# A hybrid decoder layer: low parts of weights kept in DRAM, more raw tiles at the turn into down, and tiles of its own for a layer norm

## The chip, the cores and the metric

The kernel runs on one core of a Trainium2 chip (trn2). The metric is the device time of one execution in microseconds (us); the time before is the median of three executions. A TensorE matmul (PE) multiplies a 128 x 128 stationary piece of a weight by a moving tile of 128 x 512; VectorE is called DVE, ScalarE ACT, GpSimd POOL and SyncE SP. SP issues most transfers, POOL the others, each from a queue that it takes in order.

## What is computed

One layer over 2048 positions of width 1024, all in float32. A conditioning vector gives shifts, scales and gates. The mixer has two branches, a state-space scan and a gated convolution with a layer norm behind it, both fed by one input projection and joined by one output projection; a dense squared-ReLU network follows.

```python
h = rmsnorm(x, norm_mix_w) * (1 + sc_mix) + sh_mix
z, xbc, dt_raw, glu_a, glu_b = split(h @ w_in)
y = gated_rmsnorm(ssd(silu(dwconv4(xbc)), dt_raw), z)
u = dwconv31(glu_a * sigmoid(glu_b))
u = silu(layernorm(u, cf_ln_w, cf_ln_b))
x = x + g_mix * (concat([y, u]) @ w_out)
h = rmsnorm(x, norm_mlp_w) * (1 + sc_mlp) + sh_mlp
x = x + g_mlp * (square(relu(h @ w_mlp1)) @ w_mlp2)
out = rmsnorm(x, norm_final_w)
```

## The kernel before

**Products in two parts.** Every float32 matrix is split into a high and a low part that TensorE takes at its fast rate: ACT copies the raw tile into a rounded tile (hi), and DVE subtracts that from the raw tile (lo). A product is three matmuls, hi x hi, hi x lo and lo x hi, added in PSUM. `split_w` does this for a weight block: it loads 128 x 1024 values (512 KB) by SP into one of three raw tiles (wr0, wr1, wr2, in turn), has ACT write hi into one of two tiles wh (L296) and DVE write lo into one of two tiles wl (L297). The raw tile is free when DVE has done L297, a wh and a wl tile when TensorE has finished the block that used them.

**Stages.** The 2048 positions are two halves of 1024, each of two quarters of 512 (Q).
- Mixer, half 0 (to 550 us) and half 1 (to 1000 us): 36 blocks of w_in, 48 matmuls each, are multiplied with both quarters of the half (L306 to L308), the scan and the convolution run beside that. `conv_cf` filters the gated values (31 taps, DVE) and stores v to v_d in DRAM.
- Output projection (`mix`, `mix_q`), a quarter at a time: 16 blocks of w_out with 24 matmuls each (L854 to L856), the results gated and added to x. The first two quarters run from 1009 to 1190 us, the last two from 1868 to 2047 us.
- `up` of half 0 (1191 to 1500 us), `down_` of half 0 (1502 to 1867 us), quarters three and four, `up` of half 1 (2047 to 2366 us), `down7` of half 1 (2366 to 2690 us).

So every block of w_in is split twice, and every block of w_out four times.

**The layer norm of the convolution** is a generator, `ln_cf`, that other stages advance by `ln_step`. For each of four pieces of 256 positions it loads v by POOL into two tiles cu, sums them on DVE (L410 to L413), sums over the partitions on PE (L416), subtracts the mean, squares, takes the root, scales, applies ACT's silu and stores the result from the cu tiles to m_d (L435). The sums stand in tiles ca. The convolution's filter uses cu and ca as well. For half 0 `mix` takes a step per block; for half 1 `down_` does, in its last k-block, a step per m.

**up** makes seven-product combinations of 2 x 2 weight blocks (`w1_prep`): of raw tiles x and y it forms the sums s and u in tp0 and tp1 (L985 to L987), and splits the combinations (L885 is ACT's copy, L886 DVE's subtraction, L1003 to L1005 the product's matmuls). When L987 has read y, the next y is loaded into the same tile. In half 1 `keep_ops` also forms sums of the results in tiles tt and stores seven operands per unit to op_d in DRAM, by POOL.

**down7** reads those operands again (`op_raw`, two loads per operand, in the three raw tiles) and takes weight combinations of w2 from `w2_prep`, whose first sum also stands in a tile tt. Its first operands are fetched by the generator `ahead`, advanced by `up` in its last units. The eight accumulators are loaded from x2_d with each pair of product groups.

**Who sets the order.** The statements are written in this order, with generators advanced at the places named; each engine's instructions are then placed by a scheduler, so a small move in the source can move an instruction several places on its engine. `urgent` raises the priority of a split.

## Time and profile before

| what | value |
|---|---|
| median of three executions | 2706.15 us (2704.84 to 2707.09) |
| profiled execution, its own time | 2701.98 us |
| its span | 2699.8 us |
| mean granted clock of TensorE | 0.992 |
| TensorE busy | 2634.3 us, 98% |
| VectorE busy | 2181.0 us, 81% |
| ScalarE busy | 1400.4 us, 52% |
| GpSimd busy | 300.2 us, 11% |
| read from DRAM, written | 304.65 MB, 100.93 MB |

The profile is that of one execution. Its time is 4.17 us below the median. Busy time is the time in which an engine worked on an instruction; a group of instructions is named by the line of the kernel, the engine, the operation and the tiles (out<-in). A wait is put down to the instruction or transfer that came last. The granted clock is a share of full speed: 1.00 is 2.4 GHz and 0.50 is 1.2 GHz. "DMA to landing" is the time from the issue of a transfer to its last byte.

### The profile page before, as it was taken

To read this page: it belongs to the slowest core of one execution; us is meant where nothing else is said; L and a number is where in the kernel's file an instruction comes from. 1 tells how busy PE (TensorE), PEld (TensorE's weight loads), DVE (VectorE), ACT (ScalarE), POOL (GpSimd) and SP (SyncE) were. 2 spreads that over 40 slices of the span, in tenths; PEclk is the share of its full clock that TensorE was granted. 3 is DMA by queue.
4 is the path that set the end of the run, shared out by engine and by line. 5 is a ranking of instruction groups with operands and counts; after the bars stand their busy time and mean duration, and the time that the engine had idled before them with its cause. 6 is when DMAs were issued, how large, how long until landed. Compare 5 with 4: busy or idle time off the path is not lost. (4 is left out here: it accounts for less than half of the span.)

```text
span 2699.8 us, 34186 instructions
## 1 busy us (share of the span) xinstructions
PE 2634.3 (98%) x12460; PEld 2149.7 (80%) x12460; DVE 2181.0 (81%) x3368; ACT 1400.4 (52%) x2169; POOL 300.2 (11%) x469
## 2 busy tenths in 40 slices
PE   7999999999999999999999999999999999999997
PEld 4778888788788778888888888878888778778886
DVE  7889999998996668999999874466547776588886
ACT  5757546676754755546566312354336445554452
POOL 1320120030021000011011000000001222100000
PEclk9999999999999999999999999999999999999998
DMA  7463233232322356545434733355735554564541
GB/s 288 140 214 109 79 102 110 86 111 79 118 86 78 123 177 231 164 161 188 148 137 141 242 111 100 109 195 181 244 122 188 204 197 148 197 212 146 167 148 63
DMA packets 130921, 407.82 MB, mean 151 GB/s; under 512 B 15937, under 2 KB 24769, under 8 KB 130753
## 3 DMA queue, kind: packets, MB, share of 16 engines
q1 hardware_dynamic: 97728, 294.07, 32.7%
q0 software_dynamic: 33024, 111.57, 11.6%
q8 instruction: 98, 1.61, 0.2%
q14 instruction: 71, 0.57, 0.1%
HBM read 304.65 MB, written 100.93 MB: 150 GB/s over the span
## 5 line engine op out<-in xcount | busy, mean ns | idle before, releaser
L306 PE MATMUL mm<-big,wh 128*128 128x512 f32 x1024 | 411.3, 402 | 2.4 <-DVE tp L716 1.8
L308 PE MATMUL mm<-big,wl 128*128 128x512 f32 x1024 | 403.9, 394 | 0.0
L307 PE MATMUL mm<-big,wh 128*128 128x512 f32 x1024 | 400.3, 391 | 0.0
L296 ACT ACTIVATE wh<-wr 128x1024 fp32r<-128x1024 f32 x167 | 176.1, 1055 | 314.5 <-PE mm L855 114.0
L297 DVE TENSOR_TENSOR wl<-wr,wh 128x1024 fp32r<-128x1024 f32 x167 | 203.6, 1220 | 70.1 <-ACT wh L296 59.2
L306 PEld LDWEIGHTS mm<-big,wh 128*128 128x128 f32 x1024 | 192.3, 188 | 51.9 <-issue 9.2
L308 PEld LDWEIGHTS mm<-big,wl 128*128 128x128 f32 x1024 | 192.3, 188 | 43.6 <-issue 3.2
L307 PEld LDWEIGHTS mm<-big,wh 128*128 128x128 f32 x1024 | 192.4, 188 | 42.9 <-issue 4.7
L1003 PE MATMUL mm<-big,wh 128*128 128x512 f32 x536 | 212.3, 396 | 9.1 <-ACT wh L885 3.7
L1004 PE MATMUL mm<-big,wh 128*128 128x512 f32 x536 | 210.7, 393 | 0.0
L1005 PE MATMUL mm<-big,wl 128*128 128x512 f32 x532 | 207.2, 389 | 1.2 <-DVE wl L886 1.2
L856 PE MATMUL mm<-big,wl 128*128 128x512 f32 x512 | 200.1, 391 | 1.4 <-DVE wl L297 1.4
L854 PE MATMUL mm<-big,wh 128*128 128x512 f32 x512 | 200.0, 391 | 0.4 <-ACT wh L296 0.4
L855 PE MATMUL mm<-big,wh 128*128 128x512 f32 x512 | 199.3, 389 | 0.0
L1349 PE MATMUL mm<-big,wh 128*128 128x512 f32 x496 | 194.9, 393 | 0.0
L1351 PE MATMUL mm<-big,wl 128*128 128x512 f32 x496 | 194.0, 391 | 0.3 <-DVE wl L297 0.3
L1350 PE MATMUL mm<-big,wh 128*128 128x512 f32 x496 | 194.1, 391 | 0.0
L387 DVE SCALAR_TENSOR_TENSOR ca<-cu,const,ca 128x512 f32<-128x512 f32 x240 | 178.6, 744 | 1.5 <-ACT ca L381 1.2
L390 DVE SCALAR_TENSOR_TENSOR ca<-ca,const,ca 128x512 f32<-128x512 f32 x240 | 178.3, 743 | 0.0
L1005 PE MATMUL mm<-big,wh 128*128 128x512 f32 x440 | 173.3, 394 | 0.0
L1003 PE MATMUL mm<-big,wl 128*128 128x512 f32 x436 | 170.3, 391 | 1.5 <-ACT cc L1113 1.2
L389 DVE SCALAR_TENSOR_TENSOR ca<-cu,const,ca 128x513 f32<-128x513 f32 x224 | 167.2, 746 | 3.7 <-ACT ca L383 3.7
(346 smaller groups left out, 5919.4 us busy)
## 6 DMA issues: line engine op xcount, KB each, us to landing
wr<-in_w_dram SPq DMA_DIRECT2D x120, 512.0 KB, 3.5
wr<-in_w_in_dram SPq DMA_DIRECT2D x72, 512.0 KB, 3.4
wr<-in_w_out_dram SPq DMA_DIRECT2D x64, 512.0 KB, 4.1
wr<-op_d SPq DMA_DIRECT2D x56, 512.0 KB, 4.6
ca<-in_w_ada_dram POOLq DMA_DIRECT2D x64, 256.0 KB, 3.5
tp<-ac_d SPq DMA_DIRECT2D x32, 512.0 KB, 4.3
wr<-m_d SPq DMA_DIRECT2D x32, 512.0 KB, 4.2
op_d<-tt POOLq DMA_DIRECT2D x64, 256.0 KB, 2.6
```

What stands on the lines that cost most here:

```text
L297: V.tensor_tensor(lo, raw, f(hi), SUB)
L306: T.matmul(ps, lhsT=hi[:, c], rhs=a[:, 0, :], start=(k == 0), stop=False)
L307: T.matmul(ps, lhsT=hi[:, c], rhs=a[:, 1, :], start=False, stop=False)
L308: T.matmul(ps, lhsT=lo[:, c], rhs=a[:, 0, :], start=False, stop=(k == KT - 1))
L854: T.matmul(ps, lhsT=hi[:, c], rhs=a[:, 0, :], start=(pos + k == 0), stop=False)
L855: T.matmul(ps, lhsT=hi[:, c], rhs=a[:, 1, :], start=False, stop=False)
L856: T.matmul(ps, lhsT=lo[:, c], rhs=a[:, 0, :], start=False, stop=(pos == 1 and k == KT - 1))
L1003: T.matmul(ps, lhsT=hi[:, k], rhs=xs[kp][:, 0, :], start=new and kp == 0, stop=False, skip_group_check=True)
L1004: T.matmul(ps, lhsT=hi[:, k], rhs=xs[kp][:, 1, :], start=False, stop=False, skip_group_check=True)
L1005: T.matmul(ps, lhsT=lo[:, k], rhs=xs[kp][:, 0, :], start=False, stop=kp == KP - 1, skip_group_check=True)
L1349: T.matmul(ps, lhsT=whl[0][:, c], rhs=hi, start=(k == 0), stop=False)
L1350: T.matmul(ps, lhsT=whl[0][:, c], rhs=lo, start=False, stop=False)
```

## The change

Three things are changed, and one goes with them.

1. `split_w` gets a key. At the first use of each of 52 blocks (36 of w_in, 16 of w_out) DVE makes lo as before, and POOL stores it to DRAM (lo_d). At the 84 later uses SP loads lo from there into the wl tile, in place of DVE's subtraction. The raw tile is then free when ACT has written hi.
2. The layer norm gets two tiles lv for v and two tiles la for its sums, in place of cu and ca. For half 1 its steps in `down_` come only at odd m, eight fewer, and the rest are taken by `mix` of half 1, a step per block.
3. In `w1_prep` of half 1 the sums of every second unit stand in cu0 and cu1 instead of tp0 and tp1.
4. At the turn into `down7` the raw operands have five tiles (wr0 to wr2, or0 and or1), the first operand is asked for before the first weights, and `ahead` splits three of them and asks for a fourth; the accumulators are loaded one or two at a time in another order; the first sum of `w2_prep` stands in a tile ca instead of tt.

The changed line numbers are about 15 higher: L1001 to L1003 are L985 to L987 of before, L902 is L886, L1119 and L1131 are L1103 and L1115 (DVE's part of a result of up), L989 is L974 (raw loads), L296 the raw load of `split_w`, L301 the load of lo, and L1259 the accumulator load.

Six more calls change from `split_w(w_in[b])` to `split_in(b)` (L514, L570, L581, L651, L806, L816); the rest, cut to its core:

```diff
-    def split_w(src, dst=None):
+    lo_d = {}
+    def split_w(src, dst=None, key=None):
         raw = t_wr()
...
             A.activation(hi, raw, AF.Copy)
+            if key in lo_d:
+                nc.sync.dma_start(f(lo), lo_d[key])
+                return hi, lo
             V.tensor_tensor(lo, raw, f(hi), SUB)
+        if key:
+            lo_d[key] = t_dr([P, D], f"lo_d{len(lo_d)}")
+            nc.gpsimd.dma_start(lo_d[key], f(lo))
         return hi, lo
+    def split_in(b, dst=None):
+        return split_w(w_in[b], dst, ("in", b))
...
         for j in range(2):
-            v = t_cu([P, 4, W])
+            v = t_turn("lv", 2, [P, D]).rearrange("p (a b) -> p a b", a=4)
             nc.gpsimd.dma_start(v, v_d[q // 2][:, 4 * j : 4 * j + 4, (q % 2) * 2 + i].rearrange("p k two n -> p k (two n)"))
...
             yield
-        sa = t_ca().rearrange("p (j w) -> p j w", w=W)
+        sa = t_turn("la", 2, [P, Q]).rearrange("p (j w) -> p j w", w=W)
         V.tensor_tensor(sa, vs[0][:, 0:2, :], vs[0][:, 2:4, :], ADD)
...
             V.tensor_tensor(vs[j], vs[j], mu[:, None, :].to_broadcast([P, 4, W]), SUB)
-        sq = t_ca().rearrange("p (j w) -> p j w", w=W)
+        sq = t_turn("la", 2, [P, Q]).rearrange("p (j w) -> p j w", w=W)
         for j in range(4):
...
         n = 0
-        ws = [w_out[m, pos if q % 2 else 1 - pos] for mg in (0, 4) for pos in range(2) for m in range(mg, mg + 4)]
+        ws = [(m, pos if q % 2 else 1 - pos) for mg in (0, 4) for pos in range(2) for m in range(mg, mg + 4)]
+        def weights(n):
+            return split_w(w_out[ws[n]], key=ws[n])
         if whl is None:
-            whl = split_w(ws[0])
+            whl = weights(0)
         for mg in (0, 4):
...
                     if n < 16:
-                        whl = split_w(ws[n])
+                        whl = weights(n)
                     side(n - 1)
...
             tick()
-            if half == 0:
-                ln_step(0)
+            ln_step(half)
             if n in (6, 7, 8, 9, 12, 13, 14, 15):
...
-    def w1_prep(sums0):
+    def w1_prep(half):
+        sums0 = plan[half][7]
         x, y = r2(t_raw(w1[0], "wr0")), r2(t_raw(w1[1], "wr1"))
...
                 if n == 2:
-                    s, u = (r2(t_at(t)) for t in (("tp0", "tp1") if mp else sums0))
+                    s, u = (r2(t_at(t)) for t in (sums0 if mp == 0 else ("cu0", "cu1") if half and mp % 2 else ("tp0", "tp1")))
                     V.tensor_tensor(s, y[:, 0:1, :].to_broadcast([P, 2, Q]), x, SUB)
...
         early(half, hx, second)
-        prep = w1_prep(plan[half][7])
+        prep = w1_prep(half)
         ws = [next(prep), next(prep)]
...
+        rot = [0]
         def op_raw(kb, n):
-            return [t_raw(op_d[kb][n][:, h * D : (h + 1) * D]) for h in range(2)]
+            rot[0] += 2
+            return [t_raw(op_d[kb][n][:, h * D : (h + 1) * D], ("wr0", "wr1", "wr2", "or0", "or1")[(rot[0] + h) % 5]) for h in range(2)]
...
+        def acc_load(m):
+            acc[m] = t_at(("tp7", "tp5", "tp4", "tp6", "cu0", "cu1", "state", "ac")[m])
+            nc.sync.dma_start(acc[m], x2_d[1][m])
         def ahead():
+            raws = {0: op_raw(0, 0)}
+            next(prep)
+            yield
+            raws[1] = op_raw(0, 1)
+            yield
+            op_split(0, raws[0])
+            acc_load(0)
+            acc_load(2)
+            yield
+            raws[2] = op_raw(0, 2)
             ws.extend((next(prep), next(prep)))
             yield
-            raws = op_raw(0, 0)
-            yield
-            op_split(0, raws)
+            op_split(1, raws[1])
             ws.append(next(prep))
-            raws = op_raw(0, 1)
-            yield
-            op_split(1, raws)
-            raws = op_raw(0, 2)
+            yield
+            raws[3] = op_raw(0, 3)
+            op_split(2, raws[2])
             ws.append(next(prep))
-            yield
-            op_split(2, raws)
-            raws = op_raw(0, 3)
-            yield
-            op_split(3, raws)
-            yield
+            ready.update(raws)
+            yield
+        ready = {}
...
                     for n in range(7):
-                        if kb == 0 and g == 0 and 4 <= n:
-                            op_split(n, op_raw(0, n))
+                        if kb == 0 and g == 0 and 3 <= n:
+                            op_split(n, ready[n])
+                        if kb == 0 and g == 0 and 2 <= n < 6:
+                            ready[n + 1] = ready.get(n + 1) or op_raw(0, n + 1)
+                        if kb == 0 and g == 0 and n == 0:
+                            acc_load(1)
+                            acc_load(3)
+                        if kb == 0 and g == 0 and 2 <= n < 6:
+                            acc_load(n + 2)
                         if g == 1:
...
                             mp = 2 * g + l
-                            if kb == 0 and n == 0:
-                                for m in (2 * mp, 2 * mp + 1):
-                                    acc[m] = t_at(f"tp{4 + m}" if m < 4 else ("cu0", "cu1", "state", "ac")[m - 4])
-                                    nc.sync.dma_start(acc[m], x2_d[1][m])
                             if n == 0:
...
                     src[l].update(a21=y[:, 0, :], a12=y[:, 1, :])
+                if kb == 0 and g == 0:
+                    yield
                 for n in range(7):
...
                         if n == 2:
-                            s["s1"] = t_turn("tt", 4, [P, Q])
+                            s["s1"] = t_ca()
                             V.tensor_tensor(s["s1"], s["a21"], s["a22"], SUB)
...
                     tick()
-                    if half == 0:
+                    if half == 0 and m % 2:
                         ln_step(1)
-                    if half == 0 and m % 2:
                         nxt += mix_prep(2, len(nxt), plan[1][0])
```

**SP in the third quarter of the output projection.** Before, SP's queue holds the raw loads alone (L293), each waiting for DVE, which has read the raw tile:

```order
L293 DMA wr1_2273_15389<-in_w_out_dram 128x1024 [waits DMAHW7_49,DVE_49]
L293 DMA wr2_2261_15312<-in_w_out_dram 128x1024 [waits DMAHW5_49,DVE_49]
L293 DMA wr2_2277_15434<-in_w_out_dram 128x1024 [waits DMAHW1_49,DMAHW0_49,DVE_49]
L293 DMA wr0_2281_15476<-in_w_out_dram 128x1024 [waits DMAHW4_49,DVE_49]
L293 DMA wr1_2285_15518<-in_w_out_dram 128x1024 [waits DMAHW7_49,DMAHW3_49,DVE_49]
```

Now a load of lo (L301) stands beside each raw load (L296); it waits for TensorE, the raw load for ScalarE:

```order
L296 DMA wr2_2256_15388<-in_w_out_dram 128x1024 [waits DMAHW1_49,DMAHW6_49,DVE_49,Activation_49]
L301 DMA wl1_2258_15391<-lo_d38_9289 128x1024 [waits DMAHW7_49,PE_49]
L296 DMA wr2_2277_15538<-in_w_out_dram 128x1024 [waits DMAHW6_49,DMAHW0_49,Activation_49]
L301 DMA wl0_2271_15465<-lo_d39_9322 128x1024 [waits DMAHW2_49,PE_49]
L296 DMA wr0_2281_15580<-in_w_out_dram 128x1024 [waits Activation_49]
L301 DMA wl1_2275_15496<-lo_d40_9368 128x1024 [waits DMAHW7_49,DMAHW3_49,PE_49]
```

So between two raw loads SP now waits for TensorE to give back a wl tile.

**DVE in the first units of the second up.** Before, the three sums of a unit (L985, not shown for this unit, L986 and L987) are far apart, and the L985 of the next unit follows the L987, which frees y (wr1), by four places:

```order
L986 TENSOR_TENSOR tp1_2562_17183<-wr2_2540_17066,tp0_2561_17182 128x512
...
L886 TENSOR_TENSOR tp4_2565_17191<-tp1_2562_17183,tp4_2565_17191 128x512
L1026 TENSOR_TENSOR tt1_2556_17154<-tp5_2548_17106,tt0_2555_17153 128x512
L1115 TENSOR_TENSOR cc_2560_17180<-mm2559_17167,state_2549_17110 128x512
L1028 TENSOR_TENSOR tt3_2558_17156<-tp5_2548_17106,tt1_2556_17154 128x512
L886 TENSOR_TENSOR wl1_2568_17209<-tp0_2561_17182,wl1_2568_17209 128x512
L987 TENSOR_TENSOR tp1_2562_17183<-wr1_2541_17068,tp1_2562_17183 128x512
L1115 TENSOR_TENSOR up0_2567_17207<-mm2566_17194,state_2549_17110 128x512
L1103 TENSOR_TENSOR sp1_2569_17224<-mm2559_17167,up0_2567_17207 128x512
L886 TENSOR_TENSOR wh0_2573_17233<-tp0_2561_17182,wh0_2573_17233 128x512
L985 TENSOR_TENSOR tp0_2584_17303<-wr1_2564_17189,wr0_2563_17187 128x1024
```

Now the sums stand in cu0 and cu1, and the three are within five places:

```order
L1001 TENSOR_TENSOR cu0_2561_17286<-wr1_2541_17172,wr2_2540_17170 128x1024
L1002 TENSOR_TENSOR cu1_2562_17287<-wr2_2540_17170,cu0_2561_17286 128x512
L1119 TENSOR_TENSOR sp1_2546_17207<-mm2536_17150,up1_2544_17190 128x512
L902 TENSOR_TENSOR wh0_2550_17216<-tp0_2538_17165,wh0_2550_17216 128x512
L1003 TENSOR_TENSOR cu1_2562_17287<-wr1_2541_17172,cu1_2562_17287 128x512
L1119 TENSOR_TENSOR sp2_2551_17231<-mm2543_17177,up0_2537_17163 128x512
L902 TENSOR_TENSOR wl0_2552_17235<-wr0_2524_17101,wl0_2552_17235 128x512
L1119 TENSOR_TENSOR sp0_2553_17250<-mm2536_17150,cc_2515_17064 128x512
L902 TENSOR_TENSOR wh1_2554_17254<-tp1_2539_17166,wh1_2554_17254 128x512
L1131 TENSOR_TENSOR cc_2560_17284<-mm2559_17271,state_2549_17214 128x512
```

The next L1001, which reads the next y, comes eight rows after the last one shown, 13 places behind the L1003.

**SP at the turn into the second down.** Before, after the last loads of w1, the operands of product 0 (op_d0_0) come first, into wr0 and wr1, and three raw tiles serve all:

```order
L974 DMA wr1_2843_18759<-in_w1_dram 128x1024
L974 DMA wr0_2891_19033<-op_d0_0_178 128x1024
L974 DMA wr1_2892_19035<-op_d0_0_178 128x1024
L974 DMA tp0_2884_19005<-in_w2p_dram 128x1024
L974 DMA wr2_2900_19067<-op_d0_1_179 128x1024
L974 DMA tp1_2885_19007<-in_w2p_dram 128x1024
L974 DMA tp2_2886_19009<-in_w2p_dram 128x1024
L974 DMA wr0_2901_19069<-op_d0_1_179 128x1024
L974 DMA tp3_2887_19011<-in_w2p_dram 128x1024
L974 DMA wr1_2907_19099<-op_d0_2_180 128x1024
L974 DMA wr2_2908_19101<-op_d0_2_180 128x1024
L974 DMA wr0_2915_19134<-op_d0_3_181 128x1024
```

Now the first halves of products 0 and 1 have been asked for 41 and 29 rows ahead, into or0 and or1; their second halves and product 2 stand beside the first weights of w2, with the accumulators (x2_d1) between them:

```order
L989 DMA tp0_2886_19113<-in_w2p_dram 128x1024
L989 DMA wr0_2892_19137<-op_d0_1_179 128x1024
L989 DMA tp1_2887_19115<-in_w2p_dram 128x1024
L989 DMA wr1_2902_19186<-op_d0_2_180 128x1024
L1259 DMA cu0_2935_19357<-x2_d1_4_110 128x1024
L989 DMA wr2_2884_19109<-op_d0_0_178 128x1024
L1259 DMA cu1_2944_19407<-x2_d1_5_111 128x1024
L989 DMA tp2_2888_19117<-in_w2p_dram 128x1024
L1259 DMA tp7_2899_19166<-x2_d1_0_106 128x1024
L989 DMA tp3_2889_19119<-in_w2p_dram 128x1024
L989 DMA wr2_2903_19188<-op_d0_2_180 128x1024
L989 DMA or0_2912_19241<-op_d0_3_181 128x1024
```

Product 0 is thus half fetched before the weights of the last unit of up are through, and three products' operands can lie in raw tiles at once.

## Rows read from the trace of the kernel before

**Rows 1.** The page: span, and busy time with share and instructions of each engine.
```profile
span 2699.8 us, 34186 instructions
PE 2634.3 (98%) x12460; PEld 2149.7 (80%) x12460; DVE 2181.0 (81%) x3368; ACT 1400.4 (52%) x2169; POOL 300.2 (11%) x469
```

**Rows 2.** Windows: us, then busy us (x instructions) of PE, PEld, DVE, ACT, POOL, then PEclk, DMA share, GB/s.
```profile
1550.00:1600.00 50.00, 50.00 (x222) 41.40 (x222) 44.18 (x62) 8.38 (x8) 2.25 (x3) 1.00 0.31 104
```

**Rows 3.** The page's costliest groups: busy us, mean ns; idle before, releaser.
```profile
L297 DVE TENSOR_TENSOR wl<-wr,wh 128x1024 fp32r<-128x1024 f32 x167 | 203.6, 1220 | 70.1 <-ACT wh L296 59.2
```

**Rows 4.** Waits of PE, 1780 to 1830 us: total us, times, longest us.
```profile
PE bm L416 <- DVE ca L413: 5.0, 1, 5.0
PE bm L213 <- DVE ca L427: 1.4, 1, 1.4
```

**Rows 5.** Windows at the low granted clock.
```profile
1817.60:1824.40 6.80, 4.46 (x11) 3.55 (x12) 6.34 (x10) 1.31 (x3) 0.00 (x0) 0.50 0.48 148
2158.90:2165.70 6.80, 6.09 (x15) 4.74 (x15) 3.62 (x7) 0.45 (x1) 1.61 (x3) 0.50 0.73 246
2360.30:2363.70 3.40, 3.26 (x8) 2.58 (x9) 2.32 (x5) 2.84 (x7) 0.00 (x0) 0.50 0.87 311
2384.20:2387.60 3.40, 3.40 (x8) 2.20 (x9) 3.40 (x7) 1.95 (x4) 0.00 (x0) 0.50 0.21 86
```

**Rows 6.** The chain that ended last, around 1810 us: start us, us, what.
```profile
1805.29 5.62 DMA m_d<-cu
1811.30 5.65 DMA cu<-v_d
```

**Rows 7.** Waits of PE, 2350 to 2390 us.
```profile
PE mm L1003 <- ACT wh L885: 2.8, 1, 2.8
PE mm L1003 <- ACT state L1113: 2.3, 1, 2.3
```

**Rows 8.** Timeline of ACT near 2359 us: start us, us, what, idle before.
```profile
2359.28 0.63 ACT L885 ACTIVATE big<-wr 128x512 fp32r<-128x512 f32 x1 [4.10 <-DMA wr<-op_d]
```

**Rows 9.** Windows of 2100 to 2200 us.
```profile
2100.00:2150.00 50.00, 48.52 (x211) 38.96 (x210) 37.15 (x57) 23.31 (x38) 11.90 (x22) 1.00 0.58 202
2150.00:2200.00 50.00, 46.42 (x186) 36.25 (x185) 36.22 (x55) 21.35 (x35) 11.34 (x21) 0.93 0.56 194
```

**Rows 10.** The chain around 2140 us.
```profile
2129.15 0.61 DVE tp L987
2129.78 4.93 DMA wr<-in_w_dram
2144.80 6.61 DMA wr<-in_w_dram
```

**Rows 11.** Waits of PE, 870 to 970 us.
```profile
PE sm L710 <- DVE sp L678: 2.9, 1, 2.9
PE sm L701 <- DVE sp L678: 2.3, 1, 2.3
```

**Rows 12.** Landing of the loads of L293, 1960 to 2027 us.
```profile
DMA to landing us min/median/max: 3.1/3.2/3.6
```

**Rows 13.** Landing of the loads of L293, 1895 to 1920 us.
```profile
DMA to landing us min/median/max: 5.5/5.7/5.8
```

**Rows 14.** Windows in which the queues are full.
```profile
30.00:35.00 5.00, 3.84 (x13) 2.89 (x14) 5.00 (x10) 3.45 (x5) 0.54 (x1) 0.50 1.03 414
1030.00:1050.00 20.00, 20.00 (x95) 16.70 (x93) 13.84 (x17) 12.12 (x20) 3.51 (x5) 1.00 0.90 316
1040.00:1050.00 10.00, 10.00 (x46) 8.26 (x44) 5.32 (x7) 4.75 (x8) 1.93 (x3) 1.00 0.96 353
1890.00:1930.00 40.00, 40.00 (x183) 33.23 (x181) 23.49 (x30) 14.03 (x19) 2.19 (x4) 1.00 0.82 276
1900.00:1920.00 20.00, 20.00 (x90) 16.56 (x89) 11.42 (x14) 7.29 (x12) 1.95 (x4) 1.00 0.95 320
```

**Rows 15.** DMA issues on the page: KB each, median us from issue to landing.
```profile
op_d<-tt POOLq DMA_DIRECT2D x64, 256.0 KB, 2.6
```

More of the change, by code (lines that the diff above doesn't have):

```diff
@@ L513, in tile_layer @@
                     nc.sync.dma_start(wts[sg][j], w_mod[sg, j])
-                held[W0[sg]] = split_w(w_in[W0[sg]], (d_bx(F32R), d_bx(F32R)))
+                held[W0[sg]] = split_in(W0[sg], (d_bx(F32R), d_bx(F32R)))
             x1 = load_x(1)
@@ L569, in tile_layer @@
             for n, b in enumerate(W1):
-                held[b] = split_w(w_in[b])
+                held[b] = split_in(b)
                 pre[b] = [t_mm()]
@@ L580, in tile_layer @@
         else:
-            held = {b: split_w(w_in[b]) for b in W0[:2]}
+            held = {b: split_in(b) for b in W0[:2]}
             hq = [hq0]
@@ L650, in proj @@
         def proj(blk):
-            whl = held[blk] if blk in pre else split_w(w_in[blk])
+            whl = held[blk] if blk in pre else split_in(blk)
             r = list(pre.get(blk, []))
@@ L805, in tile_layer @@
             step()
-            whl = split_w(w_in[g * 4 + 1])
+            whl = split_in(g * 4 + 1)
             for qq in range(2):
@@ L814, in tile_layer @@
                     tick()
-            whl = [split_w(w_in[g * 4 + 2]), split_w(w_in[g * 4 + 3], (d_bx(F32R), d_bx(F32R)))]
+            whl = [split_in(g * 4 + 2), split_in(g * 4 + 3, (d_bx(F32R), d_bx(F32R)))]
             for qq in range(2):
@@ L1236, in op_split @@
                 ops[n][kp] = split_x(r2(raws[kp // 2])[:, kp % 2, :], ring)
+        def acc_load(m):
+            acc[m] = t_at(("tp7", "tp5", "tp4", "tp6", "cu0", "cu1", "state", "ac")[m])
+            nc.sync.dma_start(acc[m], x2_d[1][m])
         def ahead():
+            raws = {0: op_raw(0, 0)}
[8 more added lines that the diff above has]
+            raws[2] = op_raw(0, 2)
             ws.extend((next(prep), next(prep)))
             yield
-            raws = op_raw(0, 0)
-            yield
-            op_split(0, raws)
-            ws.append(next(prep))
-            raws = op_raw(0, 1)
-            yield
-            op_split(1, raws)
-            raws = op_raw(0, 2)
+            op_split(1, raws[1])
             ws.append(next(prep))
             yield
-            op_split(2, raws)
-            raws = op_raw(0, 3)
+            raws[3] = op_raw(0, 3)
+            op_split(2, raws[2])
+            ws.append(next(prep))
+            ready.update(raws)
             yield
-            op_split(3, raws)
-            yield
+        ready = {}
         TO = ((0, 0), (0, 0), (1, 0), (1, 1), (1, 1), (1, 0), (0, 1))
```

## The prediction

> **What bounds the kernel now.** I read the head of the page first: TensorE is busy 2634.3 of 2699.8 us [rows 1], so only some 65 us can be had, and a gain has to be a named wait of TensorE or time at its lower clock. VectorE, at 2181.0 us, is behind it. The products run at one pace: in a quiet stretch 222 matmuls fill 50.00 us [rows 2], 0.225 us each, so a weight block of the output projection (24 matmuls) lasts 5.4 us and one of the input projection (48) 10.8 us. Then I read TensorE's waits, stretch by stretch, and the windows whose granted clock is 0.50 (1.2 instead of 2.4 GHz). The profiled execution took 2701.98 us, 4.17 below the median of 2706.15; all sums are made against 2701.98, and 4.17 is added at the end. About 0.2%, 5.4 us, is what a measurement of this kernel can tell from no change.
>
> **What is taken off VectorE.** 84 of the 167 subtractions of L297 go (36 of the input projection, 48 of the output projection): 84 x 1.220 us [rows 3] = 102.5 us. I cost this at nothing: in the quiet stretch VectorE works 44.18 of 50.00 us and TensorE still never waits [rows 2]. The cover is TensorE itself; what VectorE saves shows only where TensorE waits for it, and those places follow.
>
> **Gain 1, the turn of the layer norm in the first down.** Near 1815 us TensorE waits 5.0 us for the sums of L413 and 1.4 us for L427 [rows 4]. The clock then stands at 0.50 for 6.8 us: 4.46 us of work there is worth 2.23 us at full clock [rows 5]. Together 8.6 us. The chain says why: a store of m_d out of cu (5.62 us) and the load of v_d into the same cu (5.65 us) follow each other [rows 6], 11.3 us, while a step comes with every block, 5.4 us. With steps at odd m only, 10.8 us lie between them, and the last two move behind the stage. The store and load still follow each other on the two lv tiles, so a remainder of 11.3 - 10.8 = 0.5 us can show up in each of three rounds: 8.6 - 1.4, I take 7.2.
>
> **Gain 2, the turn into the second down.** Near 2360 us TensorE waits 2.8 and 2.3 us, 5.1 together [rows 7]; ScalarE had been waiting 4.10 us for a raw tile from op_d [rows 8]. The two low-clock windows hold 3.26 + 3.40 us of work at half pace, worth 3.3 us [rows 5]. Together 8.4 us. Five tiles instead of three, asked for earlier, cover the 4.10 us, but the loads and stores around it stay (311 GB/s in that stretch [rows 5]). I take 6.4, three quarters.
>
> **Gain 3, the first units of the second up.** From 2100 to 2200 us TensorE is busy 48.52 + 46.42 us [rows 9], idle 5.1 us, and a low window holds 6.09 us of work at half pace, 3.0 us lost [rows 5]: 8.1 us. The chain shows the next y tile asked for only when VectorE has done L987, then 4.93 and 6.61 us of transfer, then L985 [rows 10]. With the sums in two pairs of tiles the three subtractions stand together, and from the one that frees y to the next that needs it there are 13 places in VectorE's order instead of 4: 9 x 0.61 us = 5.5 us of lead, against 6.61 us of transfer. I take 7.0.
>
> The three give 20.6 of at most 25.1 us. In the second half of the mixer TensorE waits 2.9 and 2.3 us for L678 [rows 11], behind a VectorE that had waited for v_d. The convolution's filter moves into time that the subtractions leave, but the loads of the norm still wait for the stores out of the same two tiles. I count nothing there, and 5.2 as a bound.
>
> **What is added.** 52 stores of 512 KB (27.3 MB) and 84 loads (44.0 MB). A lo load waits for the tile that TensorE has finished two blocks before, so it has one block, plus the two matmuls before the first that reads lo: 5.4 + 0.45 = 5.85 us. With the loads spread out a raw tile lands in 3.2 us [rows 12], so in most of the 48 blocks it is hidden, and in the input projection, with 10.8 us, it is covered too. The place to look at is the third quarter, where the same loads took 5.7 us [rows 13]. From 1890 to 1930 us the queues moved 276 GB/s x 40 = 11.0 MB [rows 14]. The 7.4 blocks in it add 7.4 x 0.524 = 3.9 MB. At 353 GB/s, the best rate beside products [rows 14], 14.9 MB need 42.3 us: 2.3 too many. One more 512 KB transfer in the crowd takes 0.524 / 0.353 = 1.5 us; landing 5.7 + 1.5 = 7.2 against 5.85 leaves TensorE waiting 1.35 us in each of the 20 / 5.4 = 3.7 blocks between 1900 and 1920 us, where the queues are busy for 0.95 of the time [rows 14]: 5.0, plus half a low-clock window (1.5) = **6.5 us**. Bounds: 0, and 48 x 1.35 = 65.
>
> The Trainium skill, SBUF — State Buffer, "Summary: rules for kernel authors", puts transfers between DRAM and SBUF at about 358 GB/s; the 414 GB/s of 30 to 35 us [rows 14] is above it, so the rule is no ceiling here. By it the extra landing would be an estimated 1.46 us, by 414 GB/s 1.27, and my 6.5 would become 6.3 or 5.6.
>
> The stores of the first quarter: 1030 to 1050 us moves 316 GB/s x 20 = 6.3 MB [rows 14]; 3.7 stores add 1.9 MB, together 8.2 MB or 23.3 us at 353 GB/s, 3.3 over. A store has two blocks before its tile is rewritten, so half is hidden: **1.5** (bounds 0 and 3.3). In the mixer's second half SyncE takes its queue in order, and a lo load that waits for TensorE holds the raw load queued behind it and ScalarE's hi with that; a raw tile is asked for more than a block ahead, so I take **1** (bounds 0 and one landing, 5.7). At the start six stores of 3.1 MB join a stretch at 414 GB/s; about three fall inside it, 1.57 MB or 3.8 us, most of it behind loads asked for long before their use: **1** (bounds 0 and 3.8). POOL's queue gets 52 more issues, beside 300.2 us of work in the whole span [rows 1]; idle enough for nothing, except in rival E. The loads of the accumulators, moved in SyncE's queue, cost nothing: those of m = 1 and 3 are asked for at the first pair of products and used after the third, and a pair (24 matmuls) lasts 5.4 us.
>
> Sum: 6.5 + 1.5 + 1 + 1 = 10; -20.6 + 10 = **-10.6**. That is 2691.4 for a profiled execution, 2695.5 as a median.
>
> **Rivals.** *B, transfers have room.* If the crowd gives way, the losses fall to 2 and 3 to 7 us of the bound sum and of the mixer's waits come on top: -20.6 - 7 + 2 = -25.6, about 2680.5. For it: the loads at 3.2 us; against it: a share of 0.95 at only 320 GB/s [rows 14].
>
> *C, waits are replaced.* The stretches of gains 1 and 2 have one thing behind another: shorter waits for cu or raw tiles end in waits for the stores ahead (5.62 us each). Half of the gain, the same losses: -10.3 + 10 = -0.3, about 2706. For it: the 11.3 us of [rows 6] stay as they are.
>
> *D, the lo loads come late (slower).* The lo of every block is asked for only when TensorE is done two blocks before, and behind whatever stands ahead in SyncE's queue. At 1.35 us each it decides from (20.6 + 5.4) / 1.35 = 19 late blocks of the 48. At 24, with three low-clock windows: 24 x 1.35 + 3 x 3.0 = 41, -20.6 + 41 = +20, 2726. For it: lo has a slack of only 2.65 us over 3.2 us, where the subtraction needed none. Against it: the fourth quarter shows no crowd [rows 12].
>
> *E, POOL's queue is held up.* In the first quarter 16 lo stores are put among the loads of the norm and the stores of x2, in order. If each is held for one VectorE instruction of 1.22 us [rows 3] and half of them stand ahead of something that TensorE will need, 8 x 1.22 = 9.8 us go: -0.8, 2705.3. Against it: stores that POOL issued landed in 2.6 us [rows 15] in a stretch where VectorE was busy 36.22 of 50 us [rows 9]. It is the rule of the Trainium skill, SBUF — State Buffer, "DVE blocks DMA trap (SWDGE)", that a transfer issued by POOL cannot get its descriptors while VectorE holds the port they share, and that SyncE or ScalarE should issue it. The row of the stores does not bear it out, hence the small chance.
>
> **How the numbers follow.** Forecast .50, B .17, C .16, D .13, E .04. The forecast's own range, with gains of 16 to 25 and losses of 6 to 14, is 2687 to 2704. Faster by over 0.2% (under 2700.7): .17 of B, .46 of the forecast, .01 of C: .64. Within: .04 of the forecast, .12 of C, .03 of E: .19. Slower: D .13, C .03, E .01: .17. The range reaches into B and C and to D's near end, where 21 late blocks without a low clock give 21 x 1.35 - 20.6 = +8: 2675 to 2714. Beyond it lie most of D and the fast end of B, under 2 in 10.
>
> **What would show it.** Right: TensorE's waits at L416 and L1003 <- ScalarE gone or under 1 us, no 0.50 clock near 1820, 2160, 2360 and 2385 us; VectorE about 100 us less busy, TensorE's busy time smaller by the clock's share only. The crowd: waits of the third line of the output projection's block (L856) for a DMA into wl, in the third quarter, 5 us in all. Wrong: such waits in the fourth quarter too (D), none in the third (B), new waits at the ends of the same stretches (C), or waits for v_d loads and x2 stores in the first quarter (E).

## The result, and the profile after

The changed kernel takes 2750.06 us (median of four executions, 2741.25 to 2752.38) against 2705.49 us before: a ratio of 1.0161, 95% interval 1.0135 to 1.0187. It is slower by some 44 us, outside the range that was given. The profiled execution, at 2741.25 us, was the fastest of the four, 8.8 us below their median, so the traces can account for some 40 of the 44 us.

Its page, span and part 1, answers to [rows 1]; under it the row of VectorE's subtraction that answers to [rows 3]:

```profile
span 2739.3 us, 34315 instructions
PE 2646.9 (97%) x12460; PEld 2158.8 (79%) x12460; DVE 2089.0 (76%) x3284; ACT 1395.6 (51%) x2165; POOL 317.8 (12%) x521
```

```profile
L303 DVE TENSOR_TENSOR wl<-wr,wh 128x1024 fp32r<-128x1024 f32 x85 | 103.8, 1222 | 7.7 <-ACT wh L299 6.1
```

84 subtractions are gone (82 of them from this row, 2 from one with other tiles), VectorE is 92 us less busy, and the span is 39.5 us longer. TensorE has the same 12460 matmuls and is 12.6 us busier, which a lower clock does. Its waits (us in total, times, longest):

```profile
PE sm L543 <- DMA big<-in_w_mod_dram: 11.2, 2, 9.1
PE mm L872 <- DMA wl<-lo_d: 10.9, 7, 3.4
PE mm L872 <- DVE wl L303: 7.4, 3, 5.2
PE sm L213 <- DVE ga L242: 7.3, 3, 4.5
PE bm L428 <- DVE la L425: 5.9, 1, 5.9
PE sm L221 <- DVE rs L203: 5.7, 2, 4.8
PE mm L870 <- ACT wh L299: 4.5, 2, 2.8
PE sm L562 <- DVE ca L539: 4.3, 1, 4.3
PE mm L1019 <- ACT state L1129: 3.1, 2, 2.4
```

The first line and L562 are the start, as before. The predicted crowd is the second line. The third is the same matmul waiting for a subtraction of VectorE, in the first two quarters; the next three lie in the mixer, but for 2.3 and 0.9 us at the very end. Most waits of a few microseconds bring time at half clock. Leaving out the start and the very end there are nine such windows, against the four of [rows 5]; five are shown, with the sum over the nine:

```profile
292.40:299.20 6.80, 6.80 (x19) 5.47 (x19) 6.80 (x15) 1.76 (x3) 0.55 (x1) 0.50 0.30 68
514.30:521.10 6.80, 5.31 (x17) 4.53 (x18) 6.62 (x13) 3.36 (x6) 0.00 (x0) 0.50 0.24 81
...
985.30:992.10 6.80, 4.55 (x22) 3.53 (x23) 6.74 (x10) 0.57 (x3) 0.00 (x0) 0.50 0.43 158
1043.30:1050.20 6.90, 3.80 (x9) 3.02 (x10) 6.90 (x13) 5.20 (x7) 1.86 (x3) 0.51 0.73 220
...
2009.30:2012.70 3.40, 3.25 (x8) 2.58 (x9) 0.00 (x0) 0.00 (x0) 0.00 (x0) 0.50 0.81 330
sum 51.30, PE 42.09 PEld 33.87 DVE 44.13 ACT 20.60 POOL 5.12; mean PE 4.68 PEld 3.76 DVE 4.90 ACT 2.29 POOL 0.57
```

In them TensorE worked 42.1 us at half pace, 21.0 us lost; in the four of [rows 5] it was 17.2 us, 8.6 lost. So 12.4 of the 39.7 us by which the last matmul starts later are clock, and the rest are the waits themselves.

The predicted gains came in size. At the turn of the layer norm, 1780 to 1895 us, this is all that TensorE waits for, against [rows 4]:

```profile
PE mm L1382 <- DVE la L438: 0.6, 1, 0.6
```

At the turn into the second down the wait of 2.8 us is gone and the low clock with it, but the other wait of [rows 7] stays, as the last line of the list above (L1019 is L1003 of before), 2.4 us of it at 2406 us.

Both traces hold the same number of matmuls, so the start of the k-th in each can be set against the other's. The table gives by how many us each stretch became longer than before (minus: shorter), in the profiled execution of the change and of every experiment told of below. The times at the head are those of the kernel before; the column to 1020 us takes in the first block and more of the output projection.

| kernel | start, to 187 | mixer, to 562 | mixer, to 1020 | quarters 1, 2, to 1199 | up, down, to 1744 | turn of the norm, to 1841 | quarters 3, 4, to 2019 | up, to 2211 | turn to down, to 2402 |
|---|---|---|---|---|---|---|---|---|---|
| the change | 0.9 | **16.8** | **19.0** | **12.3** | -1.4 | -7.3 | **12.1** | -7.4 | -6.3 |
| lo_only | 8.1 | 12.1 | 6.4 | 17.8 | 1.4 | -0.4 | 8.5 | -0.8 | 1.8 |
| ln_only | 3.2 | 3.1 | 16.8 | 2.9 | 6.6 | -8.2 | 4.7 | 1.0 | 2.2 |
| turns_only | 3.6 | -1.7 | 6.5 | -0.1 | -0.4 | -0.3 | -1.2 | -6.7 | -4.9 |
| no_lo | -1.8 | 6.5 | 16.1 | 3.2 | 3.9 | -8.3 | 1.2 | -6.6 | -4.8 |
| no_store | -2.4 | 6.1 | 20.6 | 6.7 | 0.1 | -7.6 | 14.2 | -6.5 | -7.4 |
| no_load | 2.7 | 13.7 | 16.4 | 11.4 | 5.7 | -8.0 | 1.5 | -7.0 | -6.7 |
| wl4 | 5.7 | 13.8 | 18.3 | 16.5 | -0.6 | -8.3 | 5.4 | -0.8 | -5.8 |
| spaced | -0.5 | 2.0 | 5.5 | -0.9 | 0.6 | -8.2 | 0.6 | -3.1 | -7.1 |
| lv4ca | -0.4 | 2.4 | 4.8 | -0.5 | 2.9 | -8.2 | 0.3 | -6.2 | -7.1 |
| sp_store | 4.7 | 0.5 | 12.2 | 8.7 | -0.8 | -8.2 | 18.4 | -6.9 | -7.0 |
| ln_half1 | -1.9 | 2.1 | 1.7 | -0.7 | 1.4 | -8.2 | 2.1 | -6.2 | -7.7 |
| lv2ca | -2.4 | -0.4 | 4.7 | -1.8 | -0.5 | -8.2 | 2.8 | -7.2 | -7.3 |
| cu4 | -3.5 | 0.5 | 7.7 | 1.5 | -0.3 | -8.2 | -1.8 | -1.3 | -3.7 |

The gains of the change sum to 21.0 us and the losses of the four bold stretches to 60.2. Each edit also makes the scheduler place instructions anew far from the edit. turns_only, which touches nothing before 2047 us, is 6.5 us longer in the mixer's second part; so a single cell or a difference of cells is not read below some 6 us, only what several kernels share.

### The profile page after: what moved, and what is told of

Same layout as the page of the kernel before. It is cut to its first block, busy times and chain, and to the rows that moved or that the text cites. A ratio compares the mean times of both kernels' runs of the same rounds, so it can differ in the third digit from the quotient of the medians.

```text
span 2739.3 us, 34315 instructions
## 1 busy us (share of the span) xinstructions
PE 2646.9 (97%) x12460; PEld 2158.8 (79%) x12460; DVE 2089.0 (76%) x3284; ACT 1395.6 (51%) x2165; POOL 317.8 (12%) x521
## 3 DMA queue, kind: packets, MB, share of 16 engines
q0 software_dynamic: 40512, 138.83, 13.7%
## 4 chain that ended last, share of the span: by engine, by line
PE 61%; issue 11%; DMA 9%; DVE 8%; ACT 3%; POOL 2%; SPq 0%; POOLq 0%; DVEq 0%; ACTq 0%
PE mm L1019 8%; PE mm L1021 8%; PE mm L1020 8%; PE mm L318 6%; PE mm L319 5%; PE mm L320 5%; PE mm L872 3%; PE mm L870 3%; PE mm L871 3%; PE mm L1382 3%; PE mm L1383 3%; PE mm L1384 3%; DMA tp<-ac_d 2%; DMA wr<-m_d 2%; DMA lv<-v_d 1%
## 5 line engine op out<-in xcount | busy, mean ns | idle before, releaser
L320 PE MATMUL mm<-big,wl 128*128 128x512 f32 x1024 | 405.8, 396 | 0.0
L872 PE MATMUL mm<-big,wl 128*128 128x512 f32 x512 | 204.2, 399 | 18.3 <-DMA wl<-lo_d 10.9
L1019 PE MATMUL mm<-big,wh 128*128 128x512 f32 x536 | 209.6, 391 | 5.9 <-ACT state L1129 3.1
L1021 PE MATMUL mm<-big,wl 128*128 128x512 f32 x532 | 207.2, 389 | 0.6 <-DVE wl L902 0.6
L1384 PE MATMUL mm<-big,wl 128*128 128x512 f32 x496 | 193.2, 389 | 0.0
L399 DVE SCALAR_TENSOR_TENSOR ca<-cu,const,ca 128x512 f32<-128x512 f32 x240 | 179.4, 747 | 0.5 <-ACT ca L393 0.2
L402 DVE SCALAR_TENSOR_TENSOR ca<-ca,const,ca 128x512 f32<-128x512 f32 x240 | 179.5, 748 | 0.0
L1019 PE MATMUL mm<-big,wl 128*128 128x512 f32 x436 | 169.7, 389 | 0.0
L1020 PE MATMUL mm<-big,wl 128*128 128x512 f32 x436 | 169.6, 389 | 0.0
L401 DVE SCALAR_TENSOR_TENSOR ca<-cu,const,ca 128x513 f32<-128x513 f32 x224 | 168.1, 750 | 1.2 <-ACT ca L395 1.2
```

The lines of the kernel that those rows point to most:

```text
L320: T.matmul(ps, lhsT=lo[:, c], rhs=a[:, 0, :], start=False, stop=(k == KT - 1))
L872: T.matmul(ps, lhsT=lo[:, c], rhs=a[:, 0, :], start=False, stop=(pos == 1 and k == KT - 1))
L1019: T.matmul(ps, lhsT=hi[:, k], rhs=xs[kp][:, 0, :], start=new and kp == 0, stop=False, skip_group_check=True)
L1020: T.matmul(ps, lhsT=hi[:, k], rhs=xs[kp][:, 1, :], start=False, stop=False, skip_group_check=True)
L1021: T.matmul(ps, lhsT=lo[:, k], rhs=xs[kp][:, 0, :], start=False, stop=kp == KP - 1, skip_group_check=True)
L1384: T.matmul(ps, lhsT=whl[1][:, c], rhs=hi, start=False, stop=(k == FB - 1))
```

## The experiments

**Taking the three changes apart.** Four kernels, one part each or one part left out. no_lo is the changed kernel with

```diff
-        if key:
+        if False:
             lo_d[key] = t_dr([P, D], f"lo_d{len(lo_d)}")
```

lo_only is the changed kernel without the changes to `ln_cf`, the steps, `w1_prep`, `w2_prep` and `down7_of`; ln_only keeps only those to `ln_cf` and the steps; turns_only keeps only `w1_prep`, `w2_prep` and `down7_of`.

> The kernel before with the low parts of weights kept in DRAM and nothing else changed. Two theories. T1 (the stores and loads of lo cost nearly all that was lost, about 60 us by the difference of the two traces at equal matmul numbers): 2760 to 2772. T2 (the layer norm on tiles of its own costs what was lost up to the first quarter of the output projection, some 40 us, and lo only the 25 us of the output projection): 2725 to 2735.

> The kernel before with the layer norm's own tiles and its steps at odd m alone. T1: 2705 - 7 = 2698, the wait at the turn of the layer norm gone and nothing new. T2: 2705 - 7 + 30 to 40 = 2728 to 2738, with the new waits at 287, 510, 981 and 1040 us there without any lo in DRAM.

> The kernel before with the sums of w1_prep in two pairs of tiles and the five raw tiles at the turn into the second down alone. Both theories: the two steps of -7.4 and -6.3 us that the two traces show, 2705 - 13.7 = 2692.

> The changed kernel without lo in DRAM: VectorE makes it at every use, as before. T1: 2705 - 7.3 - 7.4 - 6.3 = 2684. T2: 2684 plus 30 to 40 = 2714 to 2724.

Measured: lo_only 2758.37 us (ratio 1.0181, interval 1.0153 to 1.0209), ln_only 2732.77 (1.0084, 1.0055 to 1.0112), turns_only 2696.1 (0.9947, 0.9925 to 0.9968), no_lo 2711.9 (1.0011, 0.9998 to 1.0025). Neither theory holds alone. lo_only comes just under T1's range, ln_only lies in T2's without any lo, no_lo just under T2's; turns_only is 4 us short of the gain that both forecast. The parts do not add up: lo costs some 50 us alone and 38 on top of the rest (the change against no_lo). The table says where: lo's loss lies in the mixer's first part and the four quarters, the layer norm's in the mixer's second part. Two parts of the change lose, in different places, and only the turns gain as a whole; ln_only has the 8.2 us at the turn of the norm as well.

**Stores or loads of lo.** no_store stores only the first block's lo and lets all loads read that; no_load keeps the 52 stores and lets VectorE make lo each time.

```diff
-        if key:
+        if key and lo_d:
+            lo_d[key] = next(iter(lo_d.values()))
+        elif key:
```

```diff
-            if key in lo_d:
-                nc.sync.dma_start(f(lo), lo_d[key])
-                return hi, lo
...
-        if key:
+        if key and key not in lo_d:
```

> The changed kernel with one store of lo instead of 52: all 84 loads stay and read that one block, so the products of the later uses are made with another block's low part. Theory S (the stores, on POOL's queue and in the transfer engines, cost what was lost in the first half of the mixer, 16 us, and 9 of the 13 us of the first quarter): 2750 - 25 = 2725. Theory L (the loads cost it): 2750 within 5.

> The changed kernel with all 52 stores, but VectorE makes lo at every use and no lo is loaded. Theory S: the 2712 of the kernel without lo plus 25 = 2737. Theory L: 2712, and TensorE's waits for L303 in the first quarter gone.

Measured: 2725.0 us (ratio 1.0055, 1.0035 to 1.0076) and 2731.01 (1.0074, 1.0057 to 1.0091). Theory S, and both by its figures within 6 us: without the stores the kernel is 25 us faster than the change; with the stores alone it is 19 us slower than no_lo. The loads cost as well: no_store is 13 us slower than no_lo. In the table the mixer's first part (16.8 against 6.1) belongs to the stores, quarters 3 and 4 to the loads: no_load 1.5 there, no_store 14.2. In the first two quarters (12.3 against 6.7) the difference is at the edge of what a cell can tell, but no_load has 11.4 where no_lo has 3.2.

**Who issues the stores.** A way to the loss in the mixer was read from the change's chain of waits, and led to the next experiment. POOL issues a lo store at 279.23 us; the convolution's v_d store behind it takes 5.19 us instead of 2.8, and ScalarE, which needs the tile, starts the next filter with VectorE queued behind it:

```profile
279.23 0.55 POOL lo_d L306
...
279.89 5.19 DMA v_d<-ca
285.08 0.02 issue
285.10 0.74 ACT ca L395
```

The filter's inputs, three loads of u_d into cu that POOL issues too (L372 before, L384 now), land late in the same stretch, 190 to 290 us; before, and then with the stores between them:

```profile
DMA to landing us min/median/max: 3.9/4.0/4.2
```

```profile
DMA to landing us min/median/max: 4.0/6.6/7.5
```

But no_store, which has no store of lo in this stretch, shows nearly the same:

```profile
DMA to landing us min/median/max: 3.9/5.5/7.4
```

And the chain explains little of the 4.5 us by which TensorE then waits. From 200 to 290 us VectorE stands idle for 8.9 us in the change against 2.2 before; the filter behind that v_d store has 1.2 of it. The largest part is a tile of the scan, which ScalarE makes from a load of ac_d that SyncE issues:

```profile
DVE tp L708 <- ACT tp L707: 4.1, 1, 4.1
...
DVE ca L401 <- ACT ca L395: 1.2, 1, 1.2
```

So which transfer it is that comes late is open. Whether the issuing engine matters can be tested: sp_store changes one word.

```diff
-            nc.gpsimd.dma_start(lo_d[key], f(lo))
+            nc.sync.dma_start(lo_d[key], f(lo))
```

> The changed kernel with the 52 stores of lo issued by SyncE instead of POOL. Theory Q (the stores cost by standing in POOL's queue ahead of the convolution's v_d stores, which land in 4.5 us instead of 2.8): v_d back to 2.8 to 3.2 us, the two waits near 290 and 510 us gone, 2750 - 12 to 16 = 2736. Theory T (their bytes cost, whoever issues them): 2750, v_d still above 4 us. SyncE's own queue waits for VectorE then: raw loads behind it may come late, up to 5 us against.

Measured: 2724.84 us (ratio 1.008, 1.006 to 1.0099), 25 us below the change, more than theory Q asked for; by the ratios, each measured beside the kernel before, it is 22 us, and no_store (1.0055) is 7 us faster still, with intervals that overlap. TensorE's waits from 250 to 560 us in the change, and then with SyncE's stores:

```profile
PE sm L221 <- DVE rs L203: 4.8, 1, 4.8
PE sm L213 <- DVE ga L242: 4.5, 1, 4.5
```

```profile
PE sm L221 <- DVE rs L203: 1.8, 1, 1.8
```

So the stores cost 22 to 25 us because POOL issues them; issued by SyncE, the same 27 MB cost nothing by the medians and 7 us by the ratios, which is not clear of the noise. Theory Q's sign came only in part: the v_d stores land in 3.6 us in the median of the page, not in 2.8 to 3.2, and in no_store, without the stores, in 4.0. In the mixer's first half, where the lo stores are, the eight v_d stores land in 3.0 us in the median in the change (2.8 before), and of the eight before two took over 5 us as well. So late v_d stores are not shown to be the way. The Trainium skill, DMA: Bandwidth & Descriptors, "Issuing engines are not separate DMA queues", says that issuing on several engines saves only the sequencer's time for the issue; in this case the choice of the engine is worth 22 to 25 us of the whole. A store takes 0.55 us of POOL to issue, so 52 of them take 29 us of POOL's time; whether that, the order in POOL's queue behind 512 KB of lo, or descriptors that wait for VectorE is what makes the loss, no run tells apart. The Trainium skill's rule, SBUF — State Buffer, "DVE blocks DMA trap (SWDGE)", which stood beside rival E, gives the same advice as the run, to issue from SyncE.

**More lead for the loads.** In quarters 3 and 4 of the change TensorE waits for nothing but lo; the first fence is the wait, the second the loads of lo and their landing, 1900 to 2020 us:

```profile
PE mm L872 <- DMA wl<-lo_d: 9.2, 6, 3.4
```

```profile
L301 SPq DMA_DIRECT2D wl<-lo_d x19: 319/326/424, 1904.8 to 2016.3; - x19
...
DMA to landing us min/median/max: 3.6/5.3/7.9
```

wl4 gives the weights' low parts four tiles: `t_turn("wl", 4, [P, D], F32R)`.

> The changed kernel with four wl tiles instead of two: a lo load may be asked for three blocks ahead, a store has four blocks before its tile is rewritten. If the one block of lead is what makes lo late, TensorE's 10.9 us of waits for lo loads and most of the 7.4 us for L303 go, with the clock of the third and fourth quarter: 2750 - 19 = 2731. If the transfers as such are too many, the waits stay: 2745 to 2750.

Measured: 2747.6 us (ratio 1.0141, 1.0121 to 1.0161). Half a miss. The landing is no shorter, but no wait for lo is left in that place (wl4's loads and waits, 1890 to 2130 us):

```profile
L301 SPq DMA_DIRECT2D wl<-lo_d x21: 319/327/729, 1901.7 to 2019.9; - x21
...
DMA to landing us min/median/max: 3.5/5.9/8.2
```

```profile
PE mm L870 <- DVE rs L199: 2.6, 1, 2.6
PE mm L870 <- ACT wh L299: 1.6, 2, 1.2
PE mm L1019 <- ACT wh L901: 1.0, 1, 1.0
```

So with more than one block of lead lo is no longer late, and quarters 3 and 4 went from 12.1 to 5.4 us. The total hardly moved: 6.6 us of the gain in the following up is gone (short waits for ScalarE and VectorE at 2145 us with a low-clock window), the start is 5 us longer, and L303 is still waited for in the first quarter. Which of that is the two tiles and which the new order stays open.

**Why own tiles cost 17 us in the mixer.** spaced keeps the turns and the steps at odd m, on cu and ca as before, without lo.

> The kernel before with the turns (two pairs of sum tiles, five raw tiles) and the steps of the layer norm's second half at odd m, but on the tiles cu and ca as before, and no lo in DRAM. If the spacing of the steps alone gives the 8 us at the turn of the layer norm, and the own tiles alone cost what the layer norm cost in the mixer: 2696 - 8 = 2688, faster than both kernels. If the gain needs tiles of its own: 2696.

Measured: 2693.91 us (ratio 0.9943, 0.9923 to 0.9963), faster than both kernels, but nearer to the forecast under which the gain needs own tiles. The table decides: the turn of the norm gains its 8.2 us without any tile of its own; it is the up behind it that gains less (3.1 us). The mixer's second part loses 5.5 us instead of 16 to 20, and turns_only loses 6.5 there, so of the 17 us some 11 are the own tiles'. What own tiles change there is VectorE's load. Windows of 850 to 1000 us (us, busy us of PE, PEld, DVE, ACT, POOL, then PEclk, DMA share, GB/s) of the kernel before, of the change and of no_lo:

```profile
850.00:1000.00 150.00, 144.04 (x834) 116.12 (x833) 92.81 (x155) 87.45 (x145) 9.06 (x12) 1.00 0.39 133
```

```profile
850.00:1000.00 150.00, 139.38 (x768) 111.47 (x767) 132.65 (x220) 85.33 (x140) 13.72 (x20) 0.95 0.49 160
```

```profile
850.00:1000.00 150.00, 140.24 (x792) 112.32 (x791) 135.95 (x222) 82.66 (x135) 8.31 (x11) 0.95 0.40 130
```

VectorE goes from 93 to 133 and 136 us of 150: the convolution's filter, of which the kernel before has no instruction here, runs in this stretch. And VectorE, in order, stands still for the norm's loads, as here in the first quarter of the change, 6.86 us (TensorE's longest wait for L303, 5.2 us at 1046 us, follows it):

```profile
1034.35 1.30 DVE L506 TENSOR_TENSOR big<-wr,big 128x512 fp32r<-128x512 f32 x2
1042.52 0.69 DVE L422 TENSOR_TENSOR la<-lv 128x512 f32<-128x512 f32 x1 [6.86 <-DMA lv<-v_d]
```

Two theories, then: the chain of store and load on two tiles (C) or the filter (F). Four kernels: lv4ca has four lv tiles with the sums in ca, lv2ca two lv tiles with the sums in ca, ln_half1 own tiles for the second half's norm alone, cu4 is spaced with four cu tiles.

```diff
-        sa = t_turn("la", 2, [P, Q]).rearrange("p (j w) -> p j w", w=W)
+        sa = t_ca().rearrange("p (j w) -> p j w", w=W)
...
-        sq = t_turn("la", 2, [P, Q]).rearrange("p (j w) -> p j w", w=W)
+        sq = t_ca().rearrange("p (j w) -> p j w", w=W)
```

> The changed kernel without lo in DRAM, with four lv tiles instead of two (a load of the layer norm need not wait for the store just before it) and its sums in ca. Theory C (the chain of store and load on two tiles makes VectorE stand still, and TensorE with it): the 17 us that own tiles cost in the second half of the mixer go, 2694 or, with the waits of before gone too, 2688. Theory F (own tiles let the convolution's filter run in the mixer's second half, where VectorE was 93 of 150 us busy before and 136 with own tiles, and the scan's instructions stand behind it): the loss stays, about 2712, with VectorE at 130 or more of 150 us from 850 to 1000 us.

> The two turns and the spacing of the steps, no lo in DRAM, with lv and la tiles for the second half's norm alone. If own tiles cost only where the convolution is still to be filtered: as the kernel with the spacing on cu and ca, 2694, or 2690 without the shared tiles of the third quarter; faster than both kernels. If own tiles cost wherever they are: 2705 or more.

> The changed kernel without lo in DRAM, with its two lv tiles, but the norm's sums in ca as before. Theory C (store and load on two tiles): 2712, as without lo. Theory F (the convolution's filter runs as early as free ca and cu tiles let it): about as with four lv tiles, 2683 to 2692, with VectorE near 106 of 150 us from 850 to 1000 us instead of 136.

> The kernel with the two turns and the spacing on cu and ca, no lo, but four cu tiles instead of two. Theory C: the loads of the norm need not wait for the store just before them, 2694 or up to 6 less. Theory F: more cu tiles let the filter start earlier; if VectorE rises well over 100 of 150 us from 850 to 1000 us, the loss comes back, 2700 to 2710, and if it stays near 92, 2694.

Measured: lv4ca 2682.64 us (ratio 0.9922, 0.9906 to 0.9937), ln_half1 2687.39 (0.9939, 0.9925 to 0.9953), lv2ca 2681.24 (0.9901, 0.9886 to 0.9916), cu4 2693.0 (0.9944, 0.9928 to 0.9961). lv4ca came out on theory C's side, 5 us under its 2688, and against theory F as it was first put, by which the loss stays (2712, VectorE at 130 or more; it had 106). F was then put anew, as a matter of free ca and cu tiles, and C and F made different forecasts for lv2ca: 2712, or 2683 to 2692. lv2ca, with the same two lv tiles as no_lo, is 31 us faster than it, so C falls, and the new F is 2 us off. Of the 31 us 11 lie in the mixer's second part, 7 in its first, 5 in the first two quarters. ln_half1 shows that own tiles for the second half's norm cost nothing; cu4 leaves VectorE at 90 of 150 us and tells nothing apart. lv2ca's window of 850 to 1000 us, and the filter's L401 there, first of no_lo, then of lv2ca:

```profile
850.00:1000.00 150.00, 144.39 (x822) 116.08 (x821) 108.21 (x176) 88.73 (x146) 8.32 (x11) 0.98 0.39 128
```

```profile
L401 DVE SCALAR_TENSOR_TENSOR ca<-cu,const,ca x21: 727/748/753, 853.7 to 997.6; 128x513 f32<-128x513 f32 x21
```

```profile
L401 DVE SCALAR_TENSOR_TENSOR ca<-cu,const,ca x9: 745/754/757, 989.0 to 998.2; 128x513 f32<-128x513 f32 x9
```

Twelve instructions of L401 fewer. The filter has three such lines (L399, L401, L402), 67 instructions of them in no_lo and 24 in lv2ca, 50 against 18 us; other work takes up a little, and VectorE is 28 us less busy. That the sums hold ca tiles which the filter needs fits this. VectorE stands still for the norm's loads all the same, 850 to 1060 us, in no_lo and in lv2ca:

```profile
DVE la L422 <- DMA lv<-v_d: 10.6, 3, 4.8
```

```profile
DVE ca L422 <- DMA lv<-v_d: 9.4, 2, 4.8
```

but TensorE waits for it much less (no_lo, then lv2ca, same stretch):

```profile
PE bm L428 <- DVE gra L200: 6.7, 1, 6.7
PE bm L428 <- DVE la L425: 4.1, 1, 4.1
PE sm L713 <- DVE la L438: 3.0, 1, 3.0
PE sm L713 <- DVE sp L690: 2.6, 1, 2.6
```

```profile
PE mm L870 <- ACT wh L299: 2.8, 3, 1.6
PE sm L713 <- DVE sp L690: 2.8, 1, 2.8
PE sm L722 <- DVE sp L690: 2.8, 1, 2.8
```

So the standing still hardly differs; VectorE's load around it does. Over all kernels, those with VectorE at 131 to 137 of 150 us lose 12 to 21 us in the mixer's second part, those at 86 to 108 us lose 2 to 8. That F is the whole of it isn't shown: sums in ca also move where the norm's matmul stands in TensorE's order, and every kernel of the first group has sums in tiles of their own for the first half, every one of the second has not.

lv2ca is the fastest kernel found, not told apart from lv4ca, and faster than both:

```profile
span 2679.1 us, 34174 instructions
PE 2627.6 (98%) x12460; PEld 2147.6 (80%) x12460; DVE 2182.6 (81%) x3368; ACT 1396.9 (52%) x2168; POOL 283.0 (11%) x469
```

## Why the prediction was wrong

The gains were right in size, point by point: 7.2, 7.0 and 6.4 us were forecast, 7.3, 7.4 and 6.3 came. That is closer than a cell can be read, and in part luck. Gain 1's mechanism, the spacing of the steps, is shown by spaced. Gain 3 came to anything from 0.8 us (wl4) to 7.6 us (no_store) with the same two pairs of sum tiles. In gain 2 the wait of 2.8 us lay at 2384 us, not near 2360; it went, with 3.3 us of low clock, and the wait of 2.3 us stayed, which was to go or fall under 1 us. Nothing shows that VectorE's 102 us are worth anything by themselves, as was said: no_store, with 84 loads and one store, is slower than no_lo.

What failed is the sum of the losses, 10 us against the 60.2 of the four bold stretches. Its terms measured:

- **"POOL's queue gets 52 more issues ... idle enough for nothing, except in rival E."** This is the step that failed most. The term was put at nothing, from POOL's share of busy time, and measured 22 to 25 us (sp_store), 16 of them in the mixer's first part, the two waits at 287 and 510 us for the squares of the scan's gated norm, with VectorE idle for 6.7 us more than before ahead of the first (busy 80.8 instead of 87.5 us, 200 to 290 us) and for 6.5 ahead of the second (106.1 instead of 112.6, 400 to 515 us). Rival E named the queue but looked at the first quarter alone, against a row of another stage [rows 15], and priced it at 9.8 us; its mechanism, transfers held up by VectorE, is not shown. From 240 to 560 us TensorE hardly waited before (1.1 us at most), and for that no term was put there: the absence of a wait was taken for slack. By which transfer the stores make VectorE late stays open.
- **"I count nothing there"** for the second half of the mixer. A gain of up to 5.2 us was considered there and no loss. The prediction had the filter move into time left by the subtractions; it was the norm's own tiles that moved it, and the kernels with them lose 16 to 17 us there without lo (ln_only 16.8, no_lo 16.1), some 11 more than those without them. That the idle time was what let VectorE catch up after each load of the norm fits the windows and is not shown by itself.
- **The crowd, 6.5 us in the third quarter**: right in stage and size, not in its working. The matmuls of that quarter start 6.8 us later from its first to its last block, and 5.7 us of waits of L872 for a DMA into wl lie in it, as named; but they are five waits of 0.3 to 2.6 us from 1910 to 1984 us, not 1.35 us in each block of one stretch of 20 us. "The fourth quarter shows no crowd" was nearly right: its first block waits 3.4 us, with 5.3 us lost, for a load asked for while the third quarter's crowd still ran. Behind it, 2006 to 2080 us, no load of lo is waited for:

```profile
DMA to landing us min/median/max: 3.5/3.6/5.1
```

- **Rival D's mechanism**, a lo asked for too late, is the one at work here (wl4), with 6 late blocks in quarters 3 and 4 instead of 24.
- **The first quarter's stores, 1.5 us**: lo takes about 9 of the 12.3 us of quarters 1 and 2 (no_lo 3.2). POOL's queue is only part of that: with the stores on SyncE 8.7 us are lost. In the change 7.9 of the 12.3 come where quarter 1 turns into quarter 2, and 7.0 in no_load; it is 3 there in sp_store and no_store.
- **The clock**: half a window was put into the sum; nine windows came, 12.4 us more than before. Most of the new waits carried 1.6 to 3.4 us of it with them.

The range, up to 2714, rested on 21 late loads of lo from rival D; the terms for POOL's queue and for the mixer had no upper bound that reached 20 us.

## What to carry to other kernels

Before a transfer is put on an engine's queue, list what else is issued there and who waits for that; that the queue's engine is idle nine tenths of the time is no reason to put the term at nothing, and one word that moves the transfers to another queue is a cheap experiment. An engine's idle time ahead of a bound stage may be slack for its late inputs; filling it with early work can cost more than the work that was saved. And where a scheduler places the instructions, give a change that adds tiles a term for a new order in stages that it doesn't touch, some 6 us here, and measure the parts apart: one of three paid, and the best kernel kept the turns, the spacing of the steps and half of the own tiles.

## What the runs showed of the hardware that was not expected

The 52 stores of 512 KB cost 22 to 25 us issued by POOL (sp_store against the change), and issued by SyncE, by sp_store against no_store, nothing by the medians and 7 us by the ratios, not clear of the noise. A load of 512 KB lands in 3.2 us in the median where the queues move 114 GB/s (before, 1960 to 2027 us), in 3.6 us at 205 GB/s (lo, 2006 to 2080 us), and in 5.3 us, up to 7.9, at 295 GB/s (lo, 1900 to 2020 us); before, without any lo among the loads, it was 5.7 us at 319 GB/s (1895 to 1920 us), so it goes with the crowd and not with lo. With more lead the wait went, at the same landing time. And each of the eight waits of TensorE of over 2.5 us between 280 and 2010 us of the change came with 3.4 to 6.8 us at 1.2 GHz, beginning during the wait or within 1.2 us behind it, which cost another 1.6 to 3.4 us. It is not so of every wait: in the kernel before, the 2.9 us for L678 [rows 11], at 956 us, stayed at 2.4 GHz.
